# Queries, keys and values projected 512 columns at a time in place of 256, in a two-layer attention and Hyena block

## The chip, the cores and the metric

The kernel runs on one core of one Trainium2 chip. The metric is the device time of one execution in microseconds. Matmuls run on TensorE (PE in the views, with its weight loads as PEld), elementwise work on VectorE (DVE) and ScalarE (ACT), and DMAs are issued by SyncE (SP) and GpSimd (POOL).

## The reference

Two layers of a diffusion backbone over 512 latent tokens and 256 context tokens, 1024 channels each. Per layer one input projection is cut into queries (8 heads of 128), keys and values (2 heads each), Hyena columns and gates:

```
q, k, v, hy, g = split(h @ w_in[layer])
q = apply_rope(split_heads_norm(q, q_norm[layer], 8), cos, sin)
k = apply_rope(split_heads_norm(k, k_norm[layer], 2), cos, sin)
attn = latent_attention(q, k, v, kc, vc)
x = x + gate1 * merge_branches(attn, hyena_mix(hy, ...), g, ...)
x = x + gate2 * swiglu(...)
```

Queries and keys are RMS-normalised per head; those of the latent tokens are then rotated, those of the context tokens are not. Latent queries see all 768 keys; context queries see the 256 context keys, and exist in layer 0 only. After the attention and Hyena branches are merged by gates come an output projection and a SwiGLU feed-forward.

## The kernel before, in words

All products are made of three matmuls (`mm3`, L233): an operand is split into a rounded part `hi` and a remainder `lo`, and hi·hi, hi·lo and lo·hi are summed. The split itself is a ScalarE copy (hi) and a VectorE subtraction (lo), for weights (`w_load`, L330) and for activations (`split`, L279).

**Order.** The program order of every engine is written by a class `Order`. The kernel is a set of generators; each yields what its next step needs (tiles, free slots, events), and a planner with rough costs lets the ready one with the lowest priority number go on (`go`, L156). The main program has priority 5, attention lanes 4, the gates' stores 3, the rotary 2, splits -5. What is emitted is then a fixed order per engine: an instruction that waits holds up all that stands behind it on its engine.

**Slots.** Tiles come from counted slots (L188): "s" 37, "f" 13, "ps" (the PSUM banks) 8, and for weights "raw" 5, "hi" 4, "lo" 4. "t" tiles are short-lived tiles from the "s" slots. A weight piece of 128 by 1024 numbers takes one raw, one hi and one lo slot, and it is loaded by SP only when all three are free (`w_more`, L350).

**The stage of the change.** `tok_chunk` (L916) multiplies all tokens of h by 256 weight columns: two weight pieces of four k-tiles; then for each pair of token tiles 2 x 8 x 3 matmuls with h as the stationary and the weights as the streamed operand, into the two halves of one PSUM bank; then an evacuation. A pass over 6 token tiles is 144 matmuls. The program does keys first, then values, then waits for `counts[0]` (L1316), which is hit when the keys' last transposes are emitted, and then four passes of queries of two heads each, with gates between by `MIX` (layer 0: two gates after the first pass, one after the third; layer 1: one after the second). In layer 1 queries have 4 token tiles, since context queries aren't needed.

**Rotary.** The evacuation of keys and queries (`rope_evac`, L998) copies 512 columns out of PSUM into an "f" tile (four token tiles of 256 columns) and, for the context tiles, into a "t" tile; after the fourth and the sixth token tile a `rope_chunk` (L954) is spawned. It squares on ScalarE, then on VectorE sums, takes an inverse root in nine small steps, multiplies, rotates by four operations (latent tiles only), and TensorE transposes the result, four tiles a head, for the split into kT or qT.

**Attention.** `attn_part` (L1021) handles 256 queries of a head: scores into three PSUM banks, row maxima on VectorE, exponentials on ScalarE, transposes, the product with the values, a division. Two lanes run in layer 0 (five in layer 1), each holding two "t" tiles a unit. A unit waits for the keys, the values and the queries of its head.

Of the kernel before, what the change touches and what calls it, by code (L numbers as in the profile page):

```python
# [64 lines left out]
class Order:  # L65
    """Puts the work of several generators into one program order.

    A generator yields what its next step needs: tiles that were written, free
    slots ("tag", n) or Events. Rough costs of the instructions emitted so far
    say when these are there; of the generators that can go on, the one with  # L70
    the lowest priority number does.
    """
# [7 lines left out]
    @staticmethod  # L80
    def span(ap):
        step = ap.ap[0][0]
        lo = ap.offset % step if step else ap.offset
        return ap.tensor.name, lo, lo + 1 + sum((n - 1) * abs(st) for st, n in ap.ap[1:])
# [16 lines left out]
    def run(self, eng, cost, outs, ins, late=0.15, born=None, after=0.0):  # L101
        start = max(self.now[eng], after)
        if born is not None:
            start = max(start, self.born.get(born.tensor.name, 0.0))
        for ap in ins:
            if ap.tensor.name in self.writes:
                start = max(start, self.after(ap, eng))
        for ap in outs:
            start = max(start, self.born.get(ap.tensor.name, 0.0))
        end = start + cost  # L110
        self.now[eng] = end
        for ap in ins:
            n = ap.tensor.name
# [13 lines left out]
    def give(self, tag, i, tile_):  # L127
        self.free[tag].append((self.used.get(tile_.tensor.name, 0.0), i))
# [55 lines left out]
MIX = ((2, 0, 1, 0), (0, 1, 0, 0))  # L184
# [3 lines left out]
SLOTS = {"raw": 5, "hi": 4, "lo": 4, "s": 37, "f": 13, "ps": 8}  # L188


def hyena_body(ctx, tc, I, out):
# [7 lines left out]
    # ------------------------------------------------------------- tiles and instructions  # L199
    def new(tag, dt=F32, n=None):  # L200
        kept = tag == "s"
        od.kept += kept
        tag = {"t": "s"}.get(tag, tag)
        size = {"s": TOK, "ps": 512}.get(tag, 1024)
        p = psp if tag == "ps" else sp
        free, i = od.take(tag)
        t = p.tile([P, n or size], dt, tag=f"{tag}{i}", name=tag)
        od.born[t.tensor.name] = free
        tags[t.tensor.name] = tag, i, kept
        return t  # L210

    def drop(*tiles):
        for t in tiles:
            tag, i, kept = tags[t.tensor.name]
            od.kept -= kept
            od.give(tag, i, t)
# [89 lines left out]
    # ------------------------------------------------------------- weights, in the order of use  # L306
    plan = []
    for l in range(DEPTH):
        hy = lambda i: (I["w_hy"][l, i], KD, P)
        qkv = lambda c: [(I["w_qkv"][l, c, kq], 4, 256) for kq in range(2)]  # L310
# [4 lines left out]
        for c in (4, 5, 0, 1, 2, 3):  # L315
            plan += qkv(c)
            if c < 4:
                plan += islice(gates, MIX[l][c])
# [65 lines left out]
    # ------------------------------------------------------------- modulation  # L384
# [153 lines left out]
    # ------------------------------------------------------------- projections  # L538
# [62 lines left out]
    # ------------------------------------------------------------- hyena filters  # L601
# [45 lines left out]
    class Tabs:  # L647
        """DFT tables, two of 2 KB a slot: the odd ones stay, the even ones are swapped."""
# [114 lines left out]
    # ------------------------------------------------------------- hyena branch  # L763
# [151 lines left out]
    # ------------------------------------------------------------- q, k, v  # L915
    def tok_chunk(h, nt, evac):  # L916
        ws = []
        for i in range(2):
            ws.append((yield from w_get()))
        for t0 in range(0, nt // P, 2):  # L920
            yield [("ps", 1)]
            ps = new("ps")
            for i in range(2):
                o = ps[:, 256 * i:256 * i + 256]
                s = slice(P * (t0 + i), P * (t0 + i) + P)
                for k in range(KD):
# [71 lines left out]
    def rope_evac(l, which, rope, dst, count):  # L998
        cur = []

        def evac(ps, t0):
            if t0 == 0:
                yield [("f", 1)]
                cur.append(new("f"))
            elif t0 == 4:
                yield [("t", 1)]
                cur[0:] = [new("t")]
            c = 512 * (t0 // 2 % 2)
            act(cur[0][:, c:c + 512], ps)
            drop(ps)  # L1010
            if t0:
                od.spawn(rope_chunk(cur[0], 4 if t0 == 2 else 2, which, rope, dst, 0 if t0 == 2 else 4, count), ROPE)

        return evac
# [5 lines left out]
    # ------------------------------------------------------------- attention  # L1020
# [94 lines left out]
    # ------------------------------------------------------------- layers  # L1115
# [101 lines left out]
    def program():  # L1217
# [29 lines left out]
        for l in range(DEPTH):  # L1247
# [4 lines left out]
            # norm, hyena columns  # L1252
# [5 lines left out]
            if l == 0:  # L1258
                # the residual's loads go before those of the tables
# [26 lines left out]
            # q, k, v  # L1286
# [11 lines left out]
            def v_evac(ps, t0):  # L1298
                for i in range(2):
                    split(v[0][t0 + i], v[1][t0 + i], ps[:, 256 * i:256 * i + 256], *[ps] * i)  # L1300
                if t0 == 4:
                    counts[1].hit()
                yield []
# [14 lines left out]
            for g in range(4):  # L1318
                yield [("s", 4)]
                dst = [(new("s", F32R), new("s", F32R)) for _ in range(2)]  # L1320
                qT += dst
                yield from tok_chunk(h, nt, rope_evac(l, 0, rope, dst, counts[2 + g]))
# [11 lines left out]
            # merge, output projection  # L1334
# [26 lines left out]
            # feed-forward  # L1361
# [88 lines left out]
# ---------------------------------------------------------------- host layout  # L1450
# [62 lines left out]
def _layout(i):  # L1513
# [29 lines left out]
    A["w_qkv"] = ca(qkv.reshape(DEPTH, 2, 4, P, 6, 256).transpose(0, 4, 1, 3, 2, 5))  # L1543
# [33 lines left out]
```

## Time and profile before

| | |
|---|---|
| median of three runs | 2190.36 us (2189.72 to 2190.59) |
| profiled execution, span from the first to the last instruction | 2187.6 us; its time is not recorded beside it |
| mean granted TensorE clock | 0.993 |
| projections of layer 0: keys, values, queries | first at 260.8 us |
| the same in layer 1 | first at 1440.7 us |

The page lists busy time by engine, the chain of work that ended last, and groups of instructions by line and operation, with output and inputs by the program's names: `ps<-hi,s` are the projections of the change (weights hi streamed against h in an "s" tile), `ps<-s,hi` gates and others with the weights stationary, `ps<-ident,f` transposes of rotated tiles. The timeline gives start and duration in us. Durations of matmuls overlap, so the price of one is the step from start to start.

### The profile page before, as it was taken

To read this page: it belongs to the slowest core of one execution; us is meant where nothing else is said; L and a number is where in the kernel's file an instruction comes from. 1 tells how busy PE (TensorE), PEld (TensorE's weight loads), DVE (VectorE), ACT (ScalarE), POOL (GpSimd) and SP (SyncE) were. 2 spreads that over 40 slices of the span, in tenths; PEclk is the share of its full clock that TensorE was granted. 3 is DMA by queue.
4 is the path that set the end of the run, shared out by engine and by line. 5 is a ranking of instruction groups with operands and counts; after the bars stand their busy time and mean duration, and the time that the engine had idled before them with its cause. 6 is when DMAs were issued, how large, how long until landed. Compare 5 with 4: busy or idle time off the path is not lost.

```text
span 2187.6 us, 31896 instructions
## 1 busy us (share of the span) xinstructions
PE 2146.5 (98%) x12849; PEld 1888.5 (86%) x12849; DVE 1365.3 (62%) x2510; ACT 744.3 (34%) x1350; POOL 116.8 (5%) x218
## 2 busy tenths in 40 slices
PE   7999999999999999999999999999999999999997
PEld 2889999999888888888888887899888898888887
DVE  5879766665796799733333477766756666434345
ACT  3432234444522421121221334224455443222222
POOL 2111100000100000000000011200001000000000
PEclk9999999999999999999999999999999999999999
DMA  9334521112465257812112232522213433323221
GB/s 327 100 117 151 192 81 46 37 51 80 152 229 183 78 196 239 306 44 74 65 50 82 102 111 91 182 85 73 102 49 121 158 111 99 106 83 111 80 95 57
DMA packets 83060, 256.84 MB, mean 117 GB/s; under 512 B 10668, under 2 KB 15183, under 8 KB 82912
## 3 DMA queue, kind: packets, MB, share of 16 engines
q1 hardware_dynamic: 63840, 197.43, 26.7%
q0 software_dynamic: 19072, 57.36, 8.0%
q8 instruction: 101, 1.65, 0.3%
q14 instruction: 47, 0.39, 0.1%
HBM read 232.07 MB, written 22.68 MB: 116 GB/s over the span
## 4 chain that ended last, share of the span: by engine, by line
PE 92%; DVE 4%; issue 2%; ACT 1%; DMA 1%; POOL 0%; SPq 0%; DVEq 0%; ACTq 0%; POOLq 0%
PE ps L230 89%; PE ps L240 3%; DVE s L250 1%; DVE f L254 1%; ACT s L244 1%; DVE s L254 1%; DMA s<-gated 0%; DVE mx L265 0%; DVE lo L254 0%; DMA s<-in_fw 0%; DMA f<-in_wmodf 0%; ACT hi L244 0%; ACT f L244 0%; POOL s L273 0%; DVE ss L265 0%
## 5 line engine op out<-in xcount | busy, mean ns | idle before, releaser
L230 PE MATMUL ps<-s,hi 128*128 128x512 f32 (+1 forms) x4288 | 1136.2, 353 | 7.5 <-ACT s L244 3.6
L230 PEld LDWEIGHTS ps<-s,hi 128*128 128x128 f32 x4288 | 748.5, 190 | 113.9 <-ACT s L244 4.9
L230 PE MATMUL ps<-s,lo 128*128 128x512 f32 (+1 forms) x2144 | 751.6, 351 | 1.0 <-DVE lo L254 1.0
L230 PEld LDWEIGHTS ps<-s,lo 128*128 128x128 f32 x2144 | 406.5, 190 | 55.5 <-DVE lo L254 1.4
L244 ACT ACTIVATE hi<-raw 128x1024 fp32r<-128x1024 f32 (+2 forms) x272 | 267.3, 994 | 354.1 <-PE ps L230 217.7
L254 DVE TENSOR_TENSOR lo<-raw,hi 128x1024 fp32r<-128x1024 f32 (+2 forms) x272 | 308.0, 1142 | 48.8 <-ACT hi L244 46.8
L230 PE MATMUL ps<-f,hi 128*128 128x512 f32 (+1 forms) x1184 | 297.0, 341 | 0.0
L250 DVE SCALAR_TENSOR_TENSOR s<-s,ps 128x512 f32<-128x512 f32 (+1 forms) x184 | 107.0, 587 | 280.1 <-ACT s L244 150.4
L244 ACT ACTIVATE s<-ps 128x512 f32<-128x512 f32 (+5 forms) x228 | 107.9, 492 | 353.5 <-PE ps L230 273.8
L230 PEld LDWEIGHTS ps<-f,hi 128*128 128x128 f32 x1184 | 205.0, 190 | 25.4
L230 PE MATMUL ps<-f,lo 128*128 128x512 f32 (+1 forms) x592 | 201.4, 340 | 0.0
L230 PE MATMUL ps<-hi,s 128*128 128x256 f32 x1024 | 191.6, 285 | 0.4 <-ACT s L244 0.4
L250 DVE SCALAR_TENSOR_TENSOR s<-ps,mod,s 128x256 f32<-128x256 f32 (+1 forms) x144 | 83.1, 586 | 154.2 <-PE ps L230 154.0
L230 PEld LDWEIGHTS ps<-hi,s 128*128 128x128 f32 x1024 | 162.0, 192 | 0.6 <-ACT s L244 0.6
L230 PE MATMUL ps<-f 128*128 128x256 f32 (+1 forms) x1014 | 145.5, 290 | 7.5 <-DMA f<-in_fw 3.9
L244 ACT ACTIVATE f<-ps 128x512 fp32r<-128x512 f32 (+2 forms) x164 | 90.2, 585 | 170.0 <-PE ps L230 127.2
L230 PE MATMUL ps<-lo,s 128*128 128x256 f32 x512 | 144.9, 283 | 0.0
L230 PEld LDWEIGHTS ps<-f 128*128 128x128 f32 (+1 forms) x1014 | 131.0, 190 | 12.4 <-DVE f L254 4.4
L244 ACT ACTIVATE s<-ps,nb 128x256 f32<-128x256 f32 (+1 forms) x144 | 80.7, 567 | 146.4 <-DVE nb L259 142.5
L244 ACT ACTIVATE s<-s 128x256 f32<-128x256 f32 (+4 forms) x161 | 76.6, 484 | 157.7 <-DVE s L250 125.3
L230 PEld LDWEIGHTS ps<-f,lo 128*128 128x128 f32 x592 | 112.2, 189 | 12.6
L254 DVE TENSOR_TENSOR f<-ps,f 128x512 fp32r<-128x512 f32 (+2 forms) x144 | 90.2, 654 | 41.2 <-ACT f L244 40.2
(119 smaller groups left out, 1858.9 us busy)
## 6 DMA issues: line engine op xcount, KB each, us to landing
raw<-in_w_gu SPq DMA_DIRECT2D x88, 512.0 KB, 3.3
raw<-in_wmodt SPq DMA_DIRECT2D x80, 512.0 KB, 4.3
raw<-in_w_down SPq DMA_DIRECT2D x48, 384.0 KB, 3.1
raw<-in_w_gate SPq DMA_DIRECT2D x32, 512.0 KB, 3.4
raw<-in_w_hy SPq DMA_DIRECT2D x24, 512.0 KB, 4.4
raw<-in_w_qkv SPq DMA_DIRECT2D x24, 512.0 KB, 3.3
raw<-in_w_out SPq DMA_DIRECT2D x24, 512.0 KB, 3.2
f<-in_tab POOLq DMA_DIRECT2D x40, 256.0 KB, 5.6
```

Of the source, the lines that this page charges most:

```text
L230: nc.tensor.matmul(out=o, lhsT=l, rhs=r, start=start, stop=stop)
L240: nc.tensor.transpose(o, x, ident[0:n, 0:n])
L244: nc.scalar.activation(out=o, in_=i, func=f, **kw)
L250: nc.vector.scalar_tensor_tensor(out=o, in0=a, scalar=s, in1=b, op0=op0, op1=op1)
L254: nc.vector.tensor_tensor(out=o, in0=a, in1=b, op=op)
```

## The change

The 1536 columns of queries, keys and values are cut into three groups of 512 in place of six of 256: keys and values together, then heads 0 to 3, then heads 4 to 7. A weight piece has two k-tiles of 512 columns, as many bytes as before. `tok_chunk` takes half of the token tiles at once (three, or two for layer 1's queries), one PSUM bank each, and goes through the four weight pieces with all of them; the pieces stay for the second half and are given back one by one in it. The evacuation is per token tile and copies 256 columns for each of the two pairs of heads, or the keys' 256 with a split of the values' 256. At token tiles 0 and 4 it asks for two "f" and two "t" tiles for queries. The gates between are now two after the first query pass and one after the second in layer 0, one after the first in layer 1. `Order` also gets a helper `name`, which changes nothing here.

```diff
-        qkv = lambda c: [(I["w_qkv"][l, c, kq], 4, 256) for kq in range(2)]
+        qkv = lambda c: [(I["w_qkv"][l, c, kq], 2, 512) for kq in range(4)]
...
     def tok_chunk(h, nt, evac):
+        nh = nt // P // 2
         ws = []
-        for i in range(2):
-            ws.append((yield from w_get()))
-        for t0 in range(0, nt // P, 2):
-            yield [("ps", 1)]
-            ps = new("ps")
-            for i in range(2):
-                o = ps[:, 256 * i:256 * i + 256]
-                s = slice(P * (t0 + i), P * (t0 + i) + P)
-                for k in range(KD):
-                    yield [h[k][0][:, s], h[k][1][:, s]]
-                    wh, wl, _ = ws[k // 4]
-                    mm3(o, h[k][0][:, s], h[k][1][:, s], wh[:, k % 4, :], wl[:, k % 4, :], k == 0, k == KD - 1)
-            yield from evac(ps, t0)
-        w_done(*ws)
+        for half in range(2):
+            yield [("ps", nh)]
+            os = [new("ps") for _ in range(nh)]
+            for kq in range(4):
+                if not half:
+                    ws.append((yield from w_get()))
+                wh, wl, _ = ws[kq]
+                for i, o in enumerate(os):
+                    t = nh * half + i
+                    s = slice(P * t, P * t + P)
+                    for kk in range(2):
+                        k = 2 * kq + kk
+                        yield [h[k][0][:, s], h[k][1][:, s]]
+                        mm3(o, h[k][0][:, s], h[k][1][:, s], wh[:, kk, :], wl[:, kk, :], k == 0, k == KD - 1)
+                if half:
+                    w_done(ws[kq])
+            for i, o in enumerate(os):
+                yield from evac(o, nh * half + i)
...
+    def rope_evac(which, rope, dst, counts, v=None):
+        n = 1 if v else 2
+        cur = []
+        def evac(ps, t):
+            if t in (0, 4):
+                tag = "t" if t else "f"
+                yield [(tag, n)]
+                cur[0:] = [new(tag) for _ in range(n)]
+            c = 256 * (t % 4)
+            for i in range(n):
+                act(cur[i][:, c:c + 256], ps[:, 256 * i:256 * i + 256])
+            if v:
+                split(v[0][t], v[1][t], ps[:, 256:512], ps)
+            else:
+                drop(ps)
+            if t in (3, 5):
+                for i in range(n):
+                    od.spawn(rope_chunk(cur[i], 4 if t == 3 else 2, which, rope, dst[i], 0 if t == 3 else 4,
+                                        counts[i]), ROPE)
...
-            yield from tok_chunk(h, TOK, rope_evac(l, 1, rope, kT, counts[0]))
-            yield from tok_chunk(h, TOK, v_evac)
+            yield from tok_chunk(h, TOK, rope_evac(1, rope, [kT], counts, v))
+            counts[1].hit()
...
-            for g in range(4):
-                yield [("s", 4)]
+            for g in range(2):
+                yield [("s", 8)]
```

Three places of the engines' orders follow, as the planner wrote them. On TensorE in layer 0, this is where the transposes of the rotated keys stand before the change (`ps<-ident,f` for the four latent tiles, `ps<-ident,s` for the two context tiles):

```order
L230 MATMUL ps<-lo,s 128x256
L230 MATMUL ps<-hi,s 128x256
L240 MATMUL ps<-ident,f 128x128 x8
L230 MATMUL ps<-hi,s 128x256
...
L230 MATMUL ps<-hi,s 128x256
L240 MATMUL ps<-ident,s 128x128 x4
L230 MATMUL ps<-hi,s 128x256
```

And with the change:

```order
L234 MATMUL ps<-lo,s 128x512
L234 MATMUL ps<-hi,s 128x512
L244 MATMUL ps<-ident,f 128x128 x8
L244 MATMUL ps<-ident,s 128x128 x4
L234 MATMUL ps<-hi,s 128x512
```

Before, the transposes lie inside the values' matmuls, 51 after the keys' last and 51 apart; with the change all twelve lie between the last matmul of keys and values and the first of the queries. In layer 1 the rows are the same.

On VectorE, this is what stands ahead of the keys' rotary in layer 0, from its first sum (`ss<-f`), before the change:

```order
L452 ISA mraw_91 128x1
L452 ISA raw,mraw_90<-raw,f 128x1024
L452 ISA mraw_90 128x1
L265 TENSOR_REDUCE ss<-f 128x8
L261 TENSOR_SCALAR ss<-ss 128x8
```

And with the change (`f<-ps,f` are the values' remainders, `lo<-raw,hi` those of weight pieces):

```order
L258 TENSOR_TENSOR f<-ps,f 128x256 x3
L258 TENSOR_TENSOR lo<-raw,hi 128x1024 x3
L258 TENSOR_TENSOR f<-ps,f 128x256
L258 TENSOR_TENSOR lo<-raw,hi 128x1024
L269 TENSOR_REDUCE ss<-f 128x8
L265 TENSOR_SCALAR ss<-ss 128x8
```

The remainder of the queries' fourth weight piece now stands directly ahead of the sum; that piece takes the slot that the fourth piece of keys and values holds to the end of its stage.

On TensorE in layer 0, behind the last query pass, before the change:

```order
L230 MATMUL ps<-lo,s 128x256
L230 MATMUL ps<-hi,s 128x256
L230 MATMUL ps<-f 128x256 x6
L230 MATMUL ps<-s,hi 128x512 x2
L230 MATMUL ps<-s,lo 128x512
```

And with the change, the rows behind that pass, and those where the next gate begins:

```order
L234 MATMUL ps<-hi,s 128x512
L244 MATMUL ps<-ident,s 128x128 x8
L234 MATMUL ps<-f 128x256 x6
L244 MATMUL ps<-ident,ri 128x128 x2
...
L234 MATMUL ps<-f 128x256 x6
L244 MATMUL ps<-ident,ri 128x128 x2
L244 MATMUL ps<-ident,s 128x128 x4
L234 MATMUL ps<-s,hi 128x512 x2
```

Before, a gate (`ps<-s,hi`) follows six attention matmuls behind the pass; with the change 60 rows of attention and rotary transposes lie between, and no gate.

More of the change, by code (lines that the diff above doesn't have):

```diff
@@ L78, in __init__, with span, name @@
         self.kept = 0
-    @staticmethod
-    def span(ap):
+    def span(self, ap):
         step = ap.ap[0][0]
         lo = ap.offset % step if step else ap.offset
-        return ap.tensor.name, lo, lo + 1 + sum((n - 1) * abs(st) for st, n in ap.ap[1:])
+        hi = lo + 1 + sum((n - 1) * abs(st) for st, n in ap.ap[1:])
+        return ap.tensor.name, lo, hi
+    def name(self, ap):
+        return self.span(ap)[0]
     def ready(self, ap):
@@ L103, in run @@
         if born is not None:
-            start = max(start, self.born.get(born.tensor.name, 0.0))
+            start = max(start, self.born.get(self.name(born), 0.0))
         for ap in ins:
-            if ap.tensor.name in self.writes:
+            if self.name(ap) in self.writes:
                 start = max(start, self.after(ap, eng))
         for ap in outs:
-            start = max(start, self.born.get(ap.tensor.name, 0.0))
+            start = max(start, self.born.get(self.name(ap), 0.0))
         end = start + cost
@@ L112, in run @@
         for ap in ins:
-            n = ap.tensor.name
+            n = self.name(ap)
             self.used[n] = max(self.used.get(n, 0.0), end)
@@ L127, in give @@
     def give(self, tag, i, tile_):
-        self.free[tag].append((self.used.get(tile_.tensor.name, 0.0), i))
+        self.free[tag].append((self.used.get(self.name(tile_), 0.0), i))
     def when(self, needs):
@@ L183 @@
 ADD, NORM, NPACE = (-3, -1), (-4, 3), ((), ())
-MIX = ((2, 0, 1, 0), (0, 1, 0, 0))
+MIX = ((2, 1), (1, 0))
 EARLY = (5, 3)
@@ L188 @@
 SLOTS = {"raw": 5, "hi": 4, "lo": 4, "s": 37, "f": 13, "ps": 8}
+WIDE = {"raw": 1024, "hi": 1024, "lo": 1024, "s": TOK, "f": 1024}
 def hyena_body(ctx, tc, I, out):
@@ L203, in new @@
         tag = {"t": "s"}.get(tag, tag)
-        size = {"s": TOK, "ps": 512}.get(tag, 1024)
-        p = psp if tag == "ps" else sp
         free, i = od.take(tag)
-        t = p.tile([P, n or size], dt, tag=f"{tag}{i}", name=tag)
-        od.born[t.tensor.name] = free
-        tags[t.tensor.name] = tag, i, kept
+        pl, size = (psp, 512) if tag == "ps" else (sp, WIDE[tag])
+        t = pl.tile([P, n or size], dt, tag=f"{tag}{i}", name=tag)
+        nm = t.tensor.name
+        od.born[nm] = free
+        tags[nm] = tag, i, kept
         return t
@@ L213, in drop @@
         for t in tiles:
-            tag, i, kept = tags[t.tensor.name]
+            tag, i, kept = tags[od.name(t)]
             od.kept -= kept
@@ L314, in hyena_body @@
         plan += islice(gates, EARLY[l])
-        for c in (4, 5, 0, 1, 2, 3):
+        for c in (2, 0, 1):
             plan += qkv(c)
-            if c < 4:
+            if c < 2:
                 plan += islice(gates, MIX[l][c])
@@ L996, in rope_chunk @@
         count.hit()
-    def rope_evac(l, which, rope, dst, count):
+    def rope_evac(which, rope, dst, counts, v=None):
+        n = 1 if v else 2
         cur = []
[L1001 to L1012, printed above, removed]
+        def evac(ps, t):
[14 more added lines that the diff above has]
+                                        counts[i]), ROPE)
         return evac
@@ L1296, in program @@
             counts[1].set = False
[L1298 to L1303, printed above, removed]
-            yield from tok_chunk(h, TOK, rope_evac(l, 1, rope, kT, counts[0]))
-            yield from tok_chunk(h, TOK, v_evac)
+            yield from tok_chunk(h, TOK, rope_evac(1, rope, [kT], counts, v))
+            counts[1].hit()
             qT = []
@@ L1317, in program @@
             drop(rope[1][2])
-            for g in range(4):
-                yield [("s", 4)]
-                dst = [(new("s", F32R), new("s", F32R)) for _ in range(2)]
-                qT += dst
-                yield from tok_chunk(h, nt, rope_evac(l, 0, rope, dst, counts[2 + g]))
+            for g in range(2):
+                yield [("s", 8)]
+                dst = [[(new("s", F32R), new("s", F32R)) for _ in range(2)] for _ in range(2)]
+                qT += dst[0] + dst[1]
+                yield from tok_chunk(h, nt, rope_evac(0, rope, dst, counts[2 + 2 * g:4 + 2 * g]))
                 for j in islice(gates, MIX[l][g]):
@@ L1542, in _layout @@
     qkv = np.concatenate([pr(w[:, :, Q0:V0]), w[:, :, V0:HY0]], -1)
-    A["w_qkv"] = ca(qkv.reshape(DEPTH, 2, 4, P, 6, 256).transpose(0, 4, 1, 3, 2, 5))
+    A["w_qkv"] = ca(qkv.reshape(DEPTH, 4, 2, P, 3, 512).transpose(0, 4, 1, 3, 2, 5))
     A["w_hy"] = cols(w[:, :, HY0:G0])
```

## The prediction

> **What bounds the kernel now.** I read the head of the page first, then its chain of waits, then the stage that the change touches.
>
> ```profile
> span 2187.6 us, 31896 instructions
> PE 2146.5 (98%) x12849; PEld 1888.5 (86%) x12849; DVE 1365.3 (62%) x2510; ACT 744.3 (34%) x1350; POOL 116.8 (5%) x218
> PE 92%; DVE 4%; issue 2%; ACT 1%; DMA 1%; POOL 0%; SPq 0%; DVEq 0%; ACTq 0%; POOLq 0%
> ```
>
> TensorE is busy in 98% of the span and holds 92% of the chain that ended last. So two things alone can move the time: what TensorE has to do, and how long it stands still. The windows of the stage say how still it stands; these two are the key projection of layer 0 and the middle of its attention (columns: window, length, PE, PEld, DVE, ACT and POOL busy with counts, granted clock, DMA share, GB/s).
>
> ```profile
> 260.00:280.00 20.00, 20.00 (x169) 20.00 (x169) 12.25 (x29) 5.33 (x8) 1.63 (x4) 1.00 0.52 155
> 400.00:420.00 20.00, 19.12 (x154) 18.49 (x153) 13.83 (x33) 8.82 (x24) 0.54 (x1) 1.00 0.32 99
> ```
>
> VectorE is at about two thirds beside a full TensorE. The waits of TensorE from 320 to 520 us, over the whole of layer 0's attention, confirm it:
>
> ```profile
> PE ps L230 <- ACT s L244: 1.0, 2, 0.6
> PE ps L230 <- DVE f L254: 0.7, 1, 0.7
> PE ps L240 <- DVE s L254: 0.2, 1, 0.2
> ```
>
> That is 1.9 us in 200: the interleaving of projections, gates and attention covers nearly every latency. There is almost no wait here to win, and a good deal to lose.
>
> The time is made against this profile. Its span is 2187.6 us; the median of the three runs is 2190.36, so 2.8 us lie around the span, and I leave them as they are.
>
> **The matmuls.** The two groups of the projections that change, by form:
>
> ```profile
> L230 PE MATMUL ps<-hi,s 128*128 128x256 f32 x1024 | 191.6, 285 | 0.4 <-ACT s L244 0.4
> L230 PE MATMUL ps<-lo,s 128*128 128x256 f32 x512 | 144.9, 283 | 0.0
> ```
>
> 1536 matmuls of 256 columns become 768 of 512. Their mean durations overlap, so a price is read from start to start. Below are the first and last row of 195 projection matmuls in one stretch (keys, then values), and of 24 matmuls of a gate of 512 columns:
>
> ```profile
> 260.79 0.28 PE L230 MATMUL ps<-hi,s 128*128 128x256 f32 x1
> ...
> 284.07 0.28 PE L230 MATMUL ps<-hi,s 128*128 128x256 f32 x1
> ...
> 313.92 0.63 PE L230 MATMUL ps<-s,hi 128*128 128x512 f32 x2
> ...
> 319.16 0.39 PE L230 MATMUL ps<-s,lo 128*128 128x512 f32 x1
> ```
>
> (284.07 - 260.79) / 194 = 0.1200 us for 256 columns; (319.16 - 313.92) / 23 = 0.2278 us for 512. Two narrow ones cost 0.2400, one wide one 0.2278, so each pair gains 12.2 ns. Over 768 pairs: **-9.4 us**. In the gates the wide operand is the activations and in the projections the weights; both stream, so I take the same price, and half of it, -5, as the worse end.
> The Trainium skill, "TensorE: Matmul & The Clock Gate", part 1 on the 2.5 ns of a warm matmul, speaks against that gain: start to start is N / 2.4 GHz plus about 2.5 ns, so halving the number would give an estimated 2.5 ns a pair, 1.9 us in all, and the sum would come out 7.5 us later. The trace's 120.0 and 227.8 ns are not its 109.2 and 215.8: here each matmul carries about 13 ns, and the measurement decides.
>
> **The wait for the keys.** Before the queries the program waits for the Count of the keys' rotary, so all transposes of the rotated keys stand in TensorE's order ahead of the first query matmul. Before the change the values' 144 matmuls lie between the keys' projection and these transposes. Now keys and values end together, and the order shows the eight and the four transposes directly behind the last wide matmul, in both layers. Everything in TensorE's queue stands behind them. The rotary itself, from the timeline of VectorE and ScalarE in layer 0 (start, us, engine):
>
> ```profile
> 267.24 1.05 ACT L244 ACTIVATE hi<-raw 128x1024 fp32r<-128x1024 f32 x1
> 270.47 1.22 DVE L254 TENSOR_TENSOR lo<-raw,hi 128x1024 fp32r<-128x1024 f32 x1
> 273.14 1.06 ACT L244 ACTIVATE f<-f 128x1024 f32<-128x1024 f32 x1
> 274.24 1.22 DVE L265 TENSOR_REDUCE ss<-f 128x8 f32<-128x1024 f32 x1
> ...
> 278.77 3.69 DVE L254 TENSOR_TENSOR f<-f 128x1024 f32<-128x1024 f32 x4
> ...
> 284.64 0.68 DVE L265 TENSOR_REDUCE ss<-s 128x4 f32<-128x512 f32 x1
> ...
> 288.07 0.69 DVE L254 TENSOR_TENSOR s<-s,gqk 128x512 f32<-128x512 f32 x1
> 291.34 1.42 DVE L254 TENSOR_TENSOR f<-ps,f 128x256 fp32r<-128x256 f32 x4 [0.72 <-ACT f L244]
> ```
>
> Four token tiles take 274.24 to 282.46, 8.2 us on VectorE; the two context tiles 284.64 to 288.76, 4.1 us. Both are serial on one engine. In the new order a weight piece stands ahead of the reduce: its slot comes free with the last matmul of the stage, so its rounding on ScalarE (1.05) and its remainder on VectorE (1.2) follow that matmul. From the last matmul's start: 0.4 until it has ended (the 0.39 of the gate's row), 1.05, 1.2, 8.2, then 0.75 for two halves of the values' split (2 x 0.36 of the x4 row), 4.1: 15.7 us. TensorE does the eight transposes meanwhile, needed either way:
>
> ```profile
> 284.19 1.04 PE L240 MATMUL ps<-ident,f 128*128 128x128 f32 x8
> 284.98 0.36 PE L230 MATMUL ps<-hi,s 128*128 128x256 f32 x1
> ```
>
> 0.8 us from start to start. So TensorE stands for 14.9 us a layer, **+29.8** for two. If the piece did not hold up the chain, it would start with the fourth token tile, whose sum ends 12 wide matmuls (2.7 us) before the stage does, through a copy out of PSUM (put at 0.6) and the square (1.06): 0.6 + 1.06 + 8.2 + 4.1 - 2.7 - 0.8 = 10.5 a layer. That is the low end (+21); +33 the high one. I take the upper value because the order names the piece.
>
> **The second query pass in layer 0.** Its copy out of PSUM asks, at the fifth token tile, for two "t" slots where it asked for one. "t" comes from the 37 "s" slots: h holds 16, the eight heads' queries 16, two attention lanes two each, so one is free. One was enough before; two are not. The lanes go ahead of the program by priority, so no gate is emitted until a lane lets go. The order shows it: between the second pass and the next gate, TensorE has 104 transposes, 150 matmuls of 256 columns and 24 of 512 from seven attention units and the rotary, and nothing else. By the prices above: 104 x 0.1 + 150 x 0.12 + 24 x 0.228 = 34 us. VectorE's share of the same stretch is two rotary chunks of 8.2, and, by the means of the groups from 262 to 520 us,
>
> ```profile
> L254 DVE TENSOR_TENSOR f<-ps,f 128x512 fp32r<-128x512 f32 x37 | 24.3, 683 | 9.8 <-ACT f L244 9.5
> L265 DVE TENSOR_REDUCE mx<-ps 128x1 f32<-128x512 f32 x20 | 13.6, 680 | 0.0
> L265 DVE TENSOR_REDUCE mx<-ps 128x2 f32<-128x512 f32 x15 | 10.3, 689 | 23.0 <-PE ps L230 23.0
> L254 DVE TENSOR_TENSOR s<-ps,s 128x256 f32<-128x256 f32 x15 | 6.3, 421 | 5.4 <-ACT s L244 5.2
> L269 DVE RECIPROCAL ri<-ri 128x2 f32<-128x2 f32 x10 | 1.7, 167 | 0.3
> L254 DVE TENSOR_TENSOR ri<-sm 128x2 f32<-128x2 f32 x10 | 1.6, 161 | 17.9 <-ACT s L244 17.9
> ```
>
> 20 remainders of 512 at 0.68, 16 operations of 256 at 0.42, 8 + 7 maxima at 0.68 and 0.69, about 30 small ones at 0.165: 16.4 + 13.6 + 6.7 + 10.2 + 5 = 52 us. VectorE also waits for the exponentials in each unit, 17.9 / 10 = 1.8 us, seven times at most: up to 63 us. TensorE's order threads through this chain, so the stretch lasts 52 to 63 us and TensorE stands for 18 to 29. I take **+26**, nearer the upper end, because two lanes leave little to fill that wait. The low end lies below 18: if VectorE does ten of these 52 us while the pass still runs, 8 are left.
>
> **Layer 1.** Queries there have four token tiles, so the "t" slots don't bind. But two rotary chunks come at once: after 0.4 + 1.05 + 1.2 + 8.2 + 8.2 = 19.1 us the second pair's transposes can run, and TensorE gets to them after 24 gate and 33 query matmuls, eight transposes and three matmuls, 60 x 0.228 + 0.8 = 14.5 us: **+4.7**. Counted alike in layer 0, two gates and 15 query matmuls cover the chain, so nothing.
>
> **The clock.** TensorE has just been made to stand, and the granted clock after a stand is in the trace's start:
>
> ```profile
> 45.00:50.00 5.00, 1.01 (x4) 0.93 (x4) 4.66 (x11) 2.10 (x3) 1.50 (x3) 0.58 1.10 328
> 50.00:55.00 5.00, 4.02 (x9) 2.82 (x10) 4.96 (x8) 3.31 (x4) 0.00 (x0) 0.50 0.39 137
> 55.00:60.00 5.00, 5.00 (x14) 3.87 (x14) 4.84 (x9) 3.09 (x6) 0.00 (x0) 0.55 0.31 106
> ```
>
> It fell to half in the stand before 50 us and stayed there to about 59.5 (0.55 over five us is 4.5 at half), 9.4 us with TensorE mostly busy. At half the clock a full TensorE loses half of that time: at most 4.7 us for each of the two waits for keys, and I take 2.5, since dense queries follow: **+5**, 3 to 14 with the stretch of layer 0.
>
> Other edits have one answer. Key and query copies become twice as many and half as wide, on a ScalarE at 34% of the span; the weights' bytes are the same; the loads' order on SP shifts by a few places, with DMA at 0.52 in the first window above. Nothing for these.
>
> **Sum:** -9.4 + 29.8 + 26 + 4.7 + 5 = +56. Span 2244; with the 2.8 around it, **2246 us**. With all low ends: -9.4 + 21 + 8 + 0 + 3 = +23; with all high ones -5 + 33 + 29 + 6 + 14 = +77.
>
> **Rivals.**
> *The slots don't starve the second pass for long.* If VectorE works ahead and the lanes' units overlap well, the stretch costs 8 instead of 26: +38, 2228 us. For it: VectorE has a third of its time free in the pass before. Against: the two ropes of that stretch can't begin before the pass ends. Chance 0.17.
> *The clock stays low in the stretch.* TensorE there works in bursts, about half of the time. If half the clock is granted through the first 24 us, whose 12 us of work (the rotary's transposes and some units) then double, and the later bursts lose likewise, it costs some 12 us more: +68, 2258. For it: the half clock from 50 to 60 us came with TensorE busy. Against: VectorE sets the pace, so slow matmuls partly hide. Chance 0.15. This is the rule of the Trainium skill's "TensorE: Matmul & The Clock Gate" (part 1, the two states): a window of about 3.4 us idle throttles to 1.2 GHz, one busy releases it; the rows at 45 to 60 us agree on the halving but show a longer release.
> *The waits are hidden and the matmuls win.* The wait for keys would have to shrink from 14.9 to under 4.7 us a layer, and the stretch to nothing; then -9.4 is all, 2181. For it: copies for the first three tiles run early. Against: four tiles of rotary start only with the fourth, and the order has nothing in between. Chance 0.02.
> That the matmuls don't become wide is excluded by the order: 768 of 512 columns.
>
> **The numbers.** The forecast has 0.66. Range 2220 to 2268: it holds the forecast and the first two rivals, and leaves out the corners where all ends fall together. A measurement of this kernel can tell about 0.2% from no change. Every case but one is over 1% slower: slower 0.97, same 0.01, faster 0.02.
>
> **What would show it.** In the changed kernel's profile: wide projection matmuls 0.228 us apart; a stand of some 11 and some 4 us ahead of the keys' transposes, in each layer, released by VectorE; in layer 0 a stretch of 50 to 65 us without gate matmuls, VectorE nearly full; half the clock behind the stands. It is wrong if TensorE's waits in the two attention stages sum to under 30 us, or if the time comes out under 2200.

## The result, and the profile after

The changed kernel takes 2276.98 us (median of four runs), the kernel before 2190.48 beside it: a ratio of 1.0404, interval 1.039 to 1.0417. The ratio leaves out one run of the kernel before, a slow one of 2648.76 us. The forecast was 2246 with a range up to 2268. The direction was right, the size was not: +86.5 us in place of +56. The profiled execution took 2277.13 us with a span of 2275.3 (before 2187.6).

The head of the page after, with the chain's shares by engine:

```profile
span 2275.3 us, 30417 instructions
PE 2170.2 (95%) x12081; PEld 1870.4 (82%) x12081; DVE 1368.1 (60%) x2510; ACT 747.9 (33%) x1376; POOL 116.5 (5%) x218
PE 88%; DVE 8%; ACT 2%; issue 1%; DMA 0%; SPq 0%; DVEq 0%; ACTq 0%
```

VectorE's and ScalarE's work is what it was (1368 and 748 us against 1365 and 744), but VectorE's share of the chain went from 4% to 8%: TensorE now waits for it. TensorE's busy time grew by 24 us although it has 768 matmuls fewer; that is not more work, but for the greater part work at a lower granted clock (mean 0.973, before 0.993). With two clocks, full and half (1.00 and 0.50 in the windows below), a mean of 0.973 over 2275.3 us is 2 x 0.027 x 2275.3 = 123 us at half, against 2 x 0.007 x 2187.6 = 31 before.

Taking every matmul's step from start to start against its price at full clock splits the 87.7 us of span, to within a few us: full-speed matmul work 2097.4 to 2088.0, -9.4; stands (TensorE idle) 85.3 to 157.4, +72; matmuls stretched at half clock 6.3 to 30.8, +24.5. By stage, from a layer's first key matmul to its first output projection: layer 0 from 417.1 to 479.9 us (+62.8), layer 1 from 321.5 to 344.7 (+23.2); the part between, up to layer 1's first key matmul, changed by +2.9, the rest by -1.2.

The price of a wide projection matmul, first and last row of 17 groups of three on TensorE's timeline:

```profile
268.01 0.39 PE L234 MATMUL ps<-lo,s 128*128 128x512 f32 x1
...
279.57 0.39 PE L234 MATMUL ps<-lo,s 128*128 128x512 f32 x1
```

(279.57 - 268.01) / 51 = 0.2267 us, against the 0.2278 forecast from a gate.

The wait for the keys in layer 0, on TensorE's timeline (in brackets: idle before, and who ended it), from the last wide matmul of keys and values to the first of the queries:

```profile
292.03 0.39 PE L234 MATMUL ps<-hi,s 128*128 128x512 f32 x1
302.95 1.97 PE L244 MATMUL ps<-ident,f 128*128 128x128 f32 x8 [10.53 <-DVE f L258]
307.74 1.09 PE L244 MATMUL ps<-ident,s 128*128 128x128 f32 x4 [2.82 <-DVE s L258]
308.48 0.78 PE L234 MATMUL ps<-hi,s 128*128 128x512 f32 x1
```

A stand of 10.5 and one of 2.8 us. What lay behind them is on VectorE's timeline:

```profile
293.55 1.23 DVE L258 TENSOR_TENSOR lo<-raw,hi 128x1024 fp32r<-128x1024 f32 x1 [2.52 <-ACT hi L248]
294.69 1.21 DVE L269 TENSOR_REDUCE ss<-f 128x8 f32<-128x1024 f32 x1
```

The weight piece's remainder does stand in front of the sum and waits for ScalarE's rounding, as the order had said.

The windows behind the stand and in the stretch behind the second query pass (columns as before: PE, PEld, DVE, ACT, POOL, clock, DMA, GB/s):

```profile
295.00:300.00 5.00, 0.00 (x0) 0.00 (x0) 4.59 (x13) 1.07 (x4) 0.00 (x0) 0.73 0.34 105
300.00:305.00 5.00, 1.97 (x8) 1.57 (x8) 4.80 (x12) 0.64 (x2) 0.00 (x0) 0.50 0.00 0
305.00:310.00 5.00, 2.26 (x8) 2.00 (x9) 4.40 (x12) 1.32 (x3) 0.00 (x0) 0.50 0.00 0
310.00:315.00 5.00, 5.00 (x22) 4.06 (x21) 0.00 (x0) 0.00 (x0) 0.00 (x0) 0.90 0.00 0
420.00:440.00 20.00, 7.66 (x46) 6.71 (x45) 18.63 (x39) 5.15 (x10) 0.00 (x0) 0.68 0.14 52
440.00:460.00 20.00, 14.38 (x63) 11.76 (x62) 10.98 (x24) 8.97 (x24) 0.00 (x0) 0.67 0.00 0
460.00:480.00 20.00, 14.88 (x80) 12.91 (x79) 10.47 (x26) 7.39 (x21) 0.00 (x0) 0.80 0.00 1
480.00:500.00 20.00, 15.73 (x77) 13.49 (x78) 9.19 (x25) 9.09 (x26) 0.00 (x0) 0.74 0.00 1
```

Before, TensorE was busy for 19.4 to 20.0 us in each of these last four windows, at clock 1.00; the first two of them:

```profile
420.00:440.00 20.00, 20.00 (x144) 18.78 (x143) 14.48 (x33) 9.75 (x24) 0.00 (x0) 1.00 0.01 2
440.00:460.00 20.00, 19.42 (x129) 17.55 (x128) 15.30 (x39) 10.66 (x27) 0.54 (x1) 1.00 0.21 73
```

Now VectorE is nearly full only in the first of them, during the rotary. From 440 us on no engine is full: TensorE is busy for 72 to 79%, part of it at half clock, and VectorE for about half. The ends of the stretch on TensorE's timeline:

```profile
418.88 0.39 PE L234 MATMUL ps<-hi,s 128*128 128x512 f32 x1
419.11 1.03 PE L244 MATMUL ps<-ident,s 128*128 128x128 f32 x8
432.65 1.94 PE L244 MATMUL ps<-ident,f 128*128 128x128 f32 x8 [6.98 <-DVE f L258]
...
502.31 0.71 PE L234 MATMUL ps<-s,hi 128*128 128x512 f32 x2
```

83.2 us without a gate, for 34 us of matmuls at full clock: 49 us are lost. By the same count of steps 36 of them are stands and 13 are matmuls stretched at half clock; about 20 fall in the rotary's 28 us (up to 447.36, where the next unit's scores start) and 29 in the attention's 55. TensorE's waits in the stage (255 to 560 us; the sum over all rows is 45.6 us, before 3.0) and VectorE's idle time by group within 440 to 500 us:

```profile
PE ps L244 <- DVE f L258: 19.3, 3, 10.5
PE ps L244 <- ACT s L248: 13.9, 12, 2.6
```

```profile
L258 DVE TENSOR_TENSOR ri<-sm 128x2 f32<-128x2 f32 x4 | 0.6, 160 | 7.2 <-ACT s L248 7.2
L269 DVE TENSOR_REDUCE mx<-ps 128x2 f32<-128x512 f32 x6 | 4.1, 690 | 12.8 <-PE ps L234 12.7
```

TensorE waits for ScalarE's exponentials, VectorE for TensorE's scores, and VectorE for ScalarE again. That is a chain through three engines, not one full engine.

### The profile page after: what moved, and what is told of

Read it like the earlier page. It is cut to its first block, busy times and chain, and to the rows that moved or that the text cites. A ratio compares the mean times of both kernels' runs of the same rounds, so it can differ in the third digit from the quotient of the medians.

```text
span 2275.3 us, 30417 instructions
## 1 busy us (share of the span) xinstructions
PE 2170.2 (95%) x12081; PEld 1870.4 (82%) x12081; DVE 1368.1 (60%) x2510; ACT 747.9 (33%) x1376; POOL 116.5 (5%) x218
## 4 chain that ended last, share of the span: by engine, by line
PE 88%; DVE 8%; ACT 2%; issue 1%; DMA 0%; SPq 0%; DVEq 0%; ACTq 0%
PE ps L234 85%; PE ps L244 3%; DVE f L258 2%; DVE mx L269 1%; ACT s L248 1%; DVE s L254 1%; DVE s L258 1%; DVE lo L258 1%; DVE ss L269 1%; ACT hi L248 0%; DVE rq L258 0%; DMA s<-in_fw 0%; ACT f L248 0%; DVE rq L254 0%; DVE nb L258 0%
## 5 line engine op out<-in xcount | busy, mean ns | idle before, releaser
L248 ACT ACTIVATE s<-ps 128x256 f32<-128x256 f32 (+5 forms) x234 | 108.5, 483 | 345.8 <-PE ps L234 258.9
L234 PE MATMUL ps<-f 128*128 128x256 f32 (+1 forms) x1014 | 155.0, 299 | 12.3 <-DVE f L258 7.4
L234 PE MATMUL ps<-hi,s 128*128 128x512 f32 x512 | 166.1, 397 | 0.0
L234 PEld LDWEIGHTS ps<-f 128*128 128x128 f32 (+1 forms) x1014 | 137.2, 197 | 20.1 <-DVE f L258 10.1
L248 ACT ACTIVATE f<-ps 128x512 fp32r<-128x512 f32 (+3 forms) x184 | 91.5, 541 | 167.6 <-PE ps L234 107.6
L234 PEld LDWEIGHTS ps<-hi,s 128*128 128x128 f32 x512 | 97.8, 191 | 19.9
L269 DVE TENSOR_REDUCE mx<-ps 128x1 f32<-128x512 f32 (+1 forms) x104 | 68.5, 684 | 74.7 <-PE ps L234 74.6
```

What stands on the lines that cost most here:

```text
L234: nc.tensor.matmul(out=o, lhsT=l, rhs=r, start=start, stop=stop)
L248: nc.scalar.activation(out=o, in_=i, func=f, **kw)
L269: nc.vector.tensor_reduce(out=o, in_=a, op=op, axis=AX.X)
```

## The experiments

Twelve kernels; each ratio is to the kernel before, run beside it on the same chip (medians 2188.98 to 2190.07). The theories that the expectations name by letters: A, the losses are costs of their own and add up: the keys' wait, and the missing "t" slots that starve the second query pass; B, VectorE sets the pace of the whole stage, so time won in one place is lost in the next; C, the two attention lanes stand unless enough other matmuls lie beside them; D, only the slots and VectorE's double rotary cost; E, a good part of the stretch is the half clock.

**The keys' wait taken out (e1_keys_later).** The wait for the keys' transposes is moved behind the first query pass, so the pass's matmuls lie ahead of them.

```diff
-            yield [counts[0]]
-            drop(rope[1][2])
             for g in range(2):
...
                 yield from tok_chunk(h, nt, rope_evac(0, rope, dst, counts[2 + 2 * g:4 + 2 * g]))
+                if g == 0:
+                    yield [counts[0]]
+                    drop(rope[1][2])
```

> The change, with the wait for the keys' rotary moved behind the first query pass, so that 51 wide query matmuls (11.6 us) lie ahead of the keys' first transposes in layer 0. Theory A (the wait for keys is its own cost: 14.9 us of stand and about 1.3 us at half the clock behind it, in each layer): 277 less 32, about 2245 us. Rival B (VectorE sets the pace of the whole stage, so time won here is lost at its next late result): less than 10 us won, 2267 or more.

2244.48 us, ratio 1.0254 (1.0239 to 1.027): 32.5 us under the changed kernel. On its TensorE timeline the keys' transposes have no idle time in front of them:

```profile
302.74 1.03 PE L244 MATMUL ps<-ident,f 128*128 128x128 f32 x8
307.71 0.60 PE L244 MATMUL ps<-ident,s 128*128 128x128 f32 x4
```

They also run at full clock (1.03 and 0.60 us, in the changed kernel 1.97 and 1.09). So the keys' wait with its half clock is worth about 32 us in two layers, and over a third of the loss is explained.

**One more "s" slot (e2_one_more_slot, e3_both, e4_raw_slots).** The forecast blamed two missing "t" slots. One more "s" slot gives the second pass its two; to make room, a "raw" slot goes. e3 is this with e1's edit; e4 takes the "raw" slot alone, as a control.

```diff
-SLOTS = {"raw": 5, "hi": 4, "lo": 4, "s": 37, "f": 13, "ps": 8}
+SLOTS = {"raw": 4, "hi": 4, "lo": 4, "s": 38, "f": 13, "ps": 8}
```

> The change, with 38 s slots in place of 37 (and 4 raw slots in place of 5, to make room), so that two t slots are free when the second query pass asks for them. Theory A (the pass starves for a slot, and the stretch of 83 us holds only 34 us of matmuls): the gates follow the pass at once and about 49 us are won, about 2228 us. Rival B (VectorE sets the pace): the same rotary and attention work still has to pass VectorE, so at most 20 us are won, 2257 or more.

> Both edits of the two runs before. Theory A: the two costs are apart and add up, 2277 - 32 - 49 = about 2196 us; what is left over the 2181 that the wide matmuls alone would give is layer 1's two rotary chunks at once (about 7 to 9 us) and smaller waits. Rival B: no better than 2245.

> The change with 4 raw slots in place of 5 and nothing else: a control for the run with one more s slot. The order on TensorE is unchanged word for word, so 2277 us within 0.2% by either theory; if it moves, the raw slots have a part in the other runs.

e2: 2273.78 us, 1.0385 (1.037 to 1.04). e3: 2242.22, 1.0247 (1.023 to 1.0264). e4: 2275.80, 1.0398 (1.0382 to 1.0413), so the "raw" slot is worth next to nothing. Theory A had 2228 for e2 and 2196 for e3. In the whole, the slot brought 2 to 3 us of the 49. That sum hides two effects. By stage, layer 0 gains 9.1 us (479.9 to 470.8; e3 against e1, 465.2 to 450.3) and layer 1 loses 8.1 (344.7 to 352.8; 327.8 to 335.7). In e4 layer 1 takes 344.8, so the extra slot costs this, not the "raw" one; what it changes there was not looked into. In layer 0, e2's windows tell why the gain is so small: the stretch itself is nearly full, and the stands are at the end of the attention.

```profile
420.00:440.00 20.00, 20.00 (x127) 18.02 (x126) 18.52 (x38) 8.09 (x16) 0.00 (x0) 1.00 0.17 56
...
600.00:620.00 20.00, 16.86 (x96) 14.43 (x96) 14.75 (x30) 7.11 (x17) 0.00 (x0) 0.95 0.29 89
620.00:640.00 20.00, 13.21 (x67) 11.17 (x65) 15.82 (x34) 7.32 (x21) 0.00 (x0) 0.76 0.28 96
...
660.00:680.00 20.00, 15.53 (x78) 13.21 (x79) 18.61 (x37) 5.66 (x12) 1.61 (x3) 0.74 0.72 251
```

The starvation was real, and giving the slot removed it, but some 40 of the 49 us stayed. The gates that now fill the stretch are missing later. TensorE has its last matmuls of layer 0's attention (`ps<-ident,ri`) at 667 us, before the change at 620. This points away from the slot, to other matmuls to lay beside two lanes, whose chain is longer than their own matmuls. I call these other matmuls the cover; e5 puts them to the test.

The cover can be counted. The first scores of layer 0 start at 375.25 us with the change and at 327.70 before:

```profile
375.25 2.25 PE L234 MATMUL ps<-f,s 128*128 128x512 f32 x12
```

```profile
327.70 4.37 PE L230 MATMUL ps<-f,s 128*128 128x512 f32 x24
```

That is 115.6 and 66.9 us after the layer's first key matmul, for with 512 columns a unit's queries come later, and its keys too. What then remains to be laid beside the attention: before, 432 query matmuls x 0.12 = 51.8 us, and nine gates. A gate has 24 matmuls of 512 columns and 24 of 256: 24 x 0.2278 + 24 x 0.12 = 8.35 us. So 51.8 + 75 = 127 us. With the change, 90 wide ones x 0.2278 = 20.5, and 75: 96 us. 31 us of cover are gone. (The matmuls that follow the gates are the same in both.)

**The same loss of cover in the kernel before (e5_before_less_cover).** The kernel before, with four more gates ahead of the projections: 33 us less cover, nothing else.

```diff
-EARLY = (5, 3)
+EARLY = (9, 3)
```

> The kernel before, with nine of layer 0's sixteen gates ahead of the projections in place of five: no wide matmul, no new wait, only 4 x 8.4 = 33 us less of other matmuls left to lay beside the attention, about as much as the change takes away there (127 us of projections and gates stood behind the first scores before, 96 with the change). Theory C (two attention lanes stand unless other matmuls lie beside them to the end, and the change starts the attention later, with less left): 20 to 35 us slower, 2210 to 2225, with the stands at the end of layer 0's attention. Rival D (the slot's starvation and VectorE's double rotary are what costs): no change, 2190.

2221.36 us, 1.0147 (1.0132 to 1.0162): 31.7 us for 33 us less cover, without a wide matmul or a missing slot. Layer 0's stage still takes 414.5 us (before 417.1), although four gates have been taken out of it. Its windows show the same picture as the changed kernel's stretch, no engine full and the clock lowered:

```profile
600.00:620.00 20.00, 16.13 (x93) 13.39 (x93) 10.52 (x28) 7.78 (x22) 1.61 (x3) 0.89 0.25 72
620.00:640.00 20.00, 14.15 (x74) 12.15 (x73) 9.88 (x26) 8.58 (x24) 0.54 (x1) 0.83 0.09 34
```

TensorE's longest waits there, from 560 to 660 us, are again those for the exponentials:

```profile
PE ps L240 <- ACT s L244: 12.7, 10, 2.9
```

**Cover given back to the wide kernel (e6_both_more_cover, e7_more_cover_both_layers, e11_wide_balanced).** All three start from e3. e6 keeps four gates more for the attention (EARLY of layer 0 from 5 to 1), e7 also sets two gates behind layer 1's first query pass, e11 takes the middle for layer 0. The edit below is e7's against e3; e6 has its `EARLY` alone, and e11 has `EARLY = (3, 3)`.

```diff
-MIX = ((2, 1), (1, 0))
-EARLY = (5, 3)
+MIX = ((2, 1), (2, 0))
+EARLY = (1, 3)
```

> The run with the keys' wait later and one more s slot, and one gate in place of five ahead of the projections in layer 0, so that 33 us of gates more are left to lay beside the attention. Theory C: the stands at the attention's end (about 30 us) mostly go, 2242 becomes 2212 to 2220. Rival D: no change within 5 us; a cost of its own could be that the projections then wait for the long convolution, which the early gates covered.

> As the run with more cover, and in layer 1 two gates in place of one behind the first query pass (5.4 us more ahead of the second pair's rotary transposes, where TensorE stood 5.4 us). Theory C: 5 us faster than that run; rival: the same, because VectorE is then late with the next result.

> All of the change with the waits for keys later, one more s slot, two gates behind layer 1's first pass, and three early gates in layer 0 in place of one (or the five of the change). With one the projections stood 18 us for the long convolution; with five the attention's end stood some 30. Theory C: with three, 16.7 us of cover come back, the stand for the convolution shrinks to 1 or 2 us and the attention's end stands for about 10 to 15: 2212 to 2222 us, still slower than before. Rival (the planner's luck rather than cover): outside 2205 to 2230.

e6: 2237.42, 1.0222 (1.0205 to 1.0239), a miss: the stands at the attention's end are gone (from 560 us on one of 2.5 us, in e3 18.6 in all), but the early gates had themselves been cover, for the work ahead of the projections. TensorE's waits from 220 to 300 us, 13.9 in all where the kernel before has none, have this row at their head:

```profile
PE ps L234 <- ACT f L248: 13.0, 2, 6.6
```

e7: 2227.66, 1.0179 (1.0163 to 1.0196), about 10 us under e6 where 5 were expected (layer 1's stage went from 336.3 to 326.3 us). e11: 2218.81, 1.0135 (1.0119 to 1.015), inside the expected range, but not by the expected parts: TensorE waits for 9.8 us from 220 to 300 us, where 1 or 2 were expected, and for 6.9 at the attention's end, from 560 us on, where 10 to 15 were expected. A gate covers one place or the other. Three early gates beat one by 8.9 us; five were not run with this `MIX`.

**Wide keys and values alone (e8_kv_wide_alone).** Keys and values wide with their wait, queries as before the change: 256 columns, four passes, the old gates between.

```diff
-        for c in (2, 0, 1):
-            plan += qkv(c)
-            if c < 2:
-                plan += islice(gates, MIX[l][c])
+        plan += qkv(2)
+        for c in range(4):
+            plan += [(I["w_qn"][l, c, kq], 4, 256) for kq in range(2)] + list(islice(gates, MIX[l][c]))
```

> Half of the change: keys and values together in wide matmuls with the wait behind them, but queries as before, two heads a pass with narrow matmuls, the gates between as before. Theory A and C: the keys' waits and the slow clock behind them cost 32, 288 pairs give 3.5, and the attention starts as early as before in matmuls, so it has its cover: about 2219 us, and layer 0's attention shows no other stand over 4 us. If most of the loss had another source than the four-head query pass, 2250 or more.

2218.66 us, 1.0134 (1.0119 to 1.0149), as expected. The waits of TensorE over the whole of layer 0's attention (255 to 700 us) are the keys' and nothing else above 1 us:

```profile
PE ps L244 <- DVE f L258: 10.5, 1, 10.5
PE ps L244 <- DVE s L258: 3.0, 2, 2.8
PE ps L234 <- ACT s L248: 1.0, 2, 0.6
PE ps L234 <- DVE f L258: 0.7, 1, 0.7
```

With narrow queries the stretch is gone at once. This gives back the cover (432 query matmuls lie behind the first scores again) and the slots together, so it does not tell the two apart. The time is 29 us over the kernel before; with the 3.5 us that 288 pairs gain, the keys' waits cost some 32, as e1 had it.

**Towards the best of both (e9_kv_wide_keys_later, e10_and_layer1_wide).** e9 is e8 with e1's edit; e10 has layer 1's queries wide too, with two gates behind the first pass.

> Half of the change without its waits: keys and values together in wide matmuls, the wait for the keys' rotary behind the first (narrow) query pass, queries as before. Theory A and C: of the 32 us of the keys' waits nothing is left, the attention keeps its cover, and 288 pairs at 12.2 ns give 3.5 us: 2186 to 2188, faster than the kernel before by 0.1 to 0.2%. Rival: some of the wait stays, because VectorE now has the keys' rotary beside the first pass's copies, and the time is 2195 or more.

> As the run before, with layer 1's queries wide as well and two gates behind their first pass: layer 1 has five lanes and four token tiles, so neither slots nor cover should bind. Theory C: 192 further pairs give 2.3 us, against 1 to 5 us of the second pair's rotary that two gates may not cover: 2184 to 2190. Rival: the four-head pass costs in layer 1 as in layer 0, 2200 or more.

e9: 2244.2, 1.0249 (1.0235 to 1.0263), a miss by 56 us. Layer 0 does what was hoped (418.1 us, before 417.1). Layer 1 takes 372.3 in place of 321.5; from 1550 to 1647 us no query or gate matmul runs, while the attention lanes run ahead without cover:

```profile
1540.00:1560.00 20.00, 16.69 (x120) 14.85 (x118) 10.40 (x31) 12.70 (x35) 0.00 (x0) 1.00 0.01 2
1560.00:1580.00 20.00, 11.31 (x57) 10.37 (x58) 17.59 (x38) 7.36 (x17) 0.00 (x0) 0.70 0.16 52
```

Which slot holds the passes back there was not identified. e10: 2194.69, 1.0024 (1.0015 to 1.0033): layer 0 419.2, layer 1 323.1 us. All large stands are gone, and the kernel is still slightly slower than the one before, and 5 us over what was expected. TensorE's waits in its two attention stages (255 to 700, and 1440 to 1760 us) begin with

```profile
PE ps L244 <- DVE s L258: 2.0, 1, 2.0
```

```profile
PE ps L244 <- DVE f L258: 2.1, 1, 2.1
```

and sum to 5.0 and 7.3 us, where the kernel before has 3.0 and 4.2: small stands take most of the 5.9 us that 480 pairs gain. No version beat the kernel before.

**Is it the half clock? (e12_busy_stretch).** The changed kernel, with useless 512-column matmuls laid into the stretch to keep TensorE busy: 24 ahead of a pair's rotary transposes, 9 or 2 ahead of a unit's. They write to a bank that is overwritten. They came to 140 (12221 matmuls in place of 12081), 32 us at full clock and not about 25.

```diff
+    def warm(o, n):
+        if hot["on"]:
+            x = hot["src"]
+            for _ in range(n):
+                nc.tensor.matmul(out=o[:, 0:512], lhsT=x[:, 0:128], rhs=x[:, 0:512], start=True, stop=True)
...
+            if n > 2 and hh == 0:
+                warm(p, 24)
...
+            warm(m, 2 if kp else 9)
```

> The change, with matmuls of 512 columns of no use laid into the gateless stretch of layer 0, where TensorE stands: 24 ahead of each pair's rotary transposes there and nine or two ahead of a unit's, into banks that the transposes overwrite. They add about 25 us of matmuls to a stretch that has some 49 us of stands; nothing else changes on any engine. Theory E (a good part of the stretch is the half clock: 45 of its 83 us were granted half, and its matmuls took 12.7 us longer for it): the clock stays up, the stretch shortens to 65 to 75 us and the time to 2262 to 2272. Rival (the two lanes' chain over VectorE and ScalarE sets the pace whatever the clock): the stretch stays at 80 to 90 us and the time at 2275 to 2285.

2278.94 us, 1.0403 (1.0389 to 1.0417): no gain.

```profile
420.00:440.00 20.00, 15.07 (x89) 12.74 (x87) 17.01 (x37) 7.15 (x15) 0.00 (x0) 1.00 0.15 53
440.00:460.00 20.00, 17.92 (x82) 14.77 (x82) 11.38 (x23) 5.77 (x15) 0.00 (x0) 0.83 0.00 1
...
480.00:500.00 20.00, 18.62 (x115) 15.47 (x114) 10.97 (x28) 9.24 (x26) 0.00 (x0) 1.00 0.00 1
```

The clock is full nearly throughout, and the stretch still lasts 84 us (420.87 to 504.8). Its attention part, from the first latent scores to the next gate, is shorter by about 5 us (50.2 against 54.9); the rotary part is longer by 5.5 (33.7 against 28.2). The added matmuls make this themselves. On VectorE the second pair's rotary is done at 443.71 + 2.53 = 446.2 us; on TensorE its transposes start at 452.86, without an idle gap, behind 24 added matmuls:

```profile
443.71 2.53 DVE L258 TENSOR_TENSOR f<-f 128x512 f32<-128x512 f32 x3
447.32 5.70 PE L289 MATMUL ps<-f 128*128 128x512 f32 x24
452.86 1.03 PE L244 MATMUL ps<-ident,f 128*128 128x128 f32 x8
```

The time and the stretch lie in the rival's range, so keeping the clock up in this way gains nothing. But theory E is neither shown nor refuted by it: without these 5.5 us the stretch could have been shorter. What the changed kernel's trace says is a bound: of the stretch's 49 us, 12.7 are matmuls stretched at half clock, and the other 36 are stands.

## Why the prediction was right or wrong, point by point

- **Matmuls, -9.4: right**, both in price (0.2267 us a wide one) and in the sum over the kernel (2097.4 to 2088.0). The Trainium skill, "TensorE: Matmul & The Clock Gate", part 1 on the 2.5 ns, would have given -1.9; here the trace's price held: from 0.1200 and 0.2278 us for 256 and 512 columns, 12.2 ns a matmul do not depend on the columns.
- **The wait for the keys, +29.8: right.** In layer 0, 16.45 us pass from the last wide matmul (292.03) to the first of the queries (308.48), 14.9 more than these matmuls take at full clock; layer 1 has the same. About 1.1 of the 14.9 is transposes at half clock. With the slow queries behind them the loss is 16.2 us in layer 0 and 16.4 in layer 1. e1, which removes both, gains 32.5.
- **Layer 1, +4.7: right in kind** (by its own figures 19.1 - 14.5 = 4.6), a stand of 4.81 us on TensorE's timeline, 5.7 from matmul to matmul, and about one more where the matmuls behind ran at half clock. A second stand near 1741 us, 4.9 with its half clock, was not foreseen.
- **The second query pass, +26: the step that failed.** It said that TensorE's order "threads through this chain, so the stretch lasts 52 to 63 us". It lasted 83.2, and 49 were lost: 36 in stands where 26 were forecast, and 13 at half clock, which the sum had counted only in its high end. The sum had added up VectorE's work as if VectorE stayed full. The work was right (18.63 + 10.98 + 10.47 + 9.19 = 49.3 us from 420 to 500, 52 counted), but VectorE was nearly full for 20 us only, and then busy for 9 to 11 us in 20: in turns with ScalarE and TensorE, each engine waited for another. The time of two lanes is that of their chain, not of the fullest engine on it.
- **Its cause was half wrong, too.** The missing slots put the stands where they were, but made only a part of them: e2 gave the slot, and layer 0 gained 9 us (15 beside e1's edit) of the 49. e5 shows what makes such stands without a missing slot: it takes 33 us of cover from the kernel before and loses 31.7. e8 gives the queries back their narrow passes, with cover and slots, and loses the stretch altogether.
- **The clock, +5: mis-sized.** About 2.4 us a layer at the keys' waits was right (1.1 of it is in the 14.9 above), but the forecast counted the stretch of layer 0 only in its high end. In all, matmuls stretched at half clock cost 24.5 us, of which 12.7 lie in that stretch. How much of the 12.7 would come back with the clock up isn't settled: e12's attention part fell by about 5 us, with useless matmuls in it.
- **The rival on the clock** (2258) was nearer than the forecast. Its 12 us at half clock in the stretch are there, 12.7; the stands beside them were 10 us longer than the forecast that it built on.
- **The range.** It was said to leave out the corners where all ends fall together; the upper one, 2187.6 + 2.8 + 77 = 2267.4, lies inside it.

The terms as measured nearly close the sum, with the gain shared by pairs (432 in layer 0, 336 in layer 1). In layer 0, 16.2 + 49 - 5.3 = 59.9 against 62.8 by stage; in layer 1, 16.4 + 6.8 + 4.9 - 4.1 = 24.0 against 23.2.

Left open: which slot starves layer 1 in e9, why the extra slot costs layer 1 8 us, how the last 5 us of e10 arise beyond the small stands, and the share of the half clock in the stretch, which is at most about 13 of 49 us.

## What to carry to other kernels

When a chain of dependent steps through several engines runs beside independent matmuls, count the cover: the matmuls still to be laid beside it when it can first start. A change that makes stages wider starts the chain later and uses cover up before it; in e5, 33 us less cost 32 us, over three times what the wider matmuls gave. And a stretch with few lanes is costed by the length of one unit's chain through all its engines, not by the busiest engine's sum; mending the slot at which it stood won 9 us of 49 in its layer here, and moved most of the rest to the end. A wait that can be moved behind other matmuls is another matter: e1 moved the keys' wait and won its 32 us.

## What the runs showed of the hardware that was not expected

- The clock follows the activity with a lag. Four windows of the changed kernel's stretch, cut where the clock changes:

```profile
448.00:454.00 6.00, 2.78 (x18) 2.21 (x17) 2.51 (x7) 2.44 (x9) 0.00 (x0) 1.00 0.01 1
454.00:461.00 7.00, 6.34 (x26) 5.52 (x25) 2.17 (x6) 2.05 (x6) 0.00 (x0) 0.52 0.00 0
461.00:465.00 4.00, 1.37 (x8) 1.02 (x6) 2.51 (x7) 0.81 (x3) 0.00 (x0) 0.93 0.00 0
465.00:471.00 6.00, 5.49 (x24) 4.98 (x24) 2.61 (x6) 3.24 (x9) 0.00 (x0) 0.50 0.01 3
```

  Full clock stands over the idle pieces and half the clock over the busy ones behind them: the burst of matmuls after a stand is what runs slowly. The Trainium skill's "TensorE: Matmul & The Clock Gate" (part 1, the two states) ties the half clock to an idle window of about 3.4 us, released by a busy one. Behind the keys' wait the trace agrees (0.50 from 300 to 310 us, 0.90 in the window from 310 on, with dense queries from 308.48). In the stretch from 440 to 500 us TensorE's longest single stand is 2.6 us, and the clock fell there too. If the transposes are left out of the count, the gaps are longer: at each of the falls, near 454, 465, 482 and 495 us, lies a gap of 3.9 to 5.0 us in which TensorE ran nothing but transposes (449.8 to 454.7, 462.2 to 467.2, 478.7 to 483.2, 490.1 to 494.0). Whether transposes keep the clock up was not tested.
- Useless matmuls laid into the stands held the clock at 1.00 in most windows (e12), and the time did not fall: 2278.94 against 2276.98 us. They stood ahead of transposes that were ready.
